# A short bias table read with overlapping rows, and forget-gated heads and pooling products over all 128 rows

## The chip, the core and the metric

The kernel runs on one core of one Trainium2 chip. The metric is the device time of one execution in microseconds (us); several runs are made, and their median counts.

## The reference, cut to what matters

The model is a chain of ten stages on 512 tokens of width 1024: an even mixer, memory cross-attention and feed-forward, then an odd mixer, cross-attention and feed-forward, and then twice a second kind of mixer (`mixer2`) with its feed-forward. The change touches three places.

The odd mixer has eight heads of dilated attention with three branches. The kernel merges them into one softmax over 512 keys, with a bias that depends on the head and on the distance between query and key alone:

```
bias = rel_bias[_t5_bucket(delta * dil)].transpose(2, 0, 1)
logits = jnp.where(valid, logits + bias, -jnp.inf)
```

In `mixer2` eight heads of 64 columns attend with forget gates, in query blocks of 128, each over the keys up to its own end:

```
logits = einsum('bhqd,bhkd->bhqk', qb, kb) * scale
logits = logits + (c[:, :, q0:q1, None] - c[:, :, None, :q1])
logits = jnp.where(causal, logits, -inf);  p = softmax(logits)
```

and four pooling groups of 64 columns each pass through a small product:

```
d = stack(groups, axis=2)                 # (b, s, 4, 64)
out = einsum('bsgc,gcd->bsgd', d, w_grp)  # 64 -> 256 per group
```

## The kernel before

All large products are float32 split in two float32r parts, a high one and a low one: `mm3` issues three products (high x high, high x low, low x high) for each 128-row piece (L246 to 251). `unit` (L206) is how weights come in: SP loads a block of 1024 columns by 128 rows into one of 3 raw buffers, ScalarE casts the high part (L167), VectorE subtracts it for the low part (L168), and the pairs have 5 buffers. SP's queue carries nearly all weight loads, in order; a load waits there until a raw buffer is free. POOL's queue carries the parked copy of X and small transfers. A scheduler orders the instructions of each engine ahead of time by its own model; each engine then runs its list in order and waits at semaphores. Products go to two PSUM tags, `mm` and `at`, with four banks each.

`bias_table` (L1110) runs in the first cross-attention (layer 0), between the products for the memory's keys and values and those for the queries. It multiplies a 33 x 640 one-hot matrix by the 33 x 8 bias rows (L1122), copies the 8 x 640 result to SBUF (L1123), and writes it to DRAM with each row repeated 128 times, one element further each time: 8 x 128 x 512. `odd_head` (L1214) reads 128 x 512 of it per head into `bt` (L1220, two buffers), and VectorE adds a slice of it to the logits and takes the maximum in one instruction (L1229).

In `mixer2` (L1248) the keys are projected first, then the queries. After each token tile `forget_k` (L1564) transposes it and writes, for even and odd heads (e = 0, 1), the high part into the 64 rows of that head and, by a copy on POOL's queue, into the other 64 rows as well. The low part goes into 64 rows of `kl` alone, even heads in one half of the rows and odd heads in the other. `forget_q` writes the query's high part into the head's own 64 rows and its low part into the other 64. So one product over 128 rows gives q_high k_high + q_low k_high, and a second one over 64 rows (L1607) gives q_high k_low. `forget_head` (L1591) adds per query block the gate sums (L1603), the causal mask as identity x mask in bfloat16 (L1604), and those two (L1606, L1607), with n = 128, 256, 384 or 512 columns, all into one bank. The head loop (L1316) issues for each head: its logits, a quarter of the short convolution's projection as filler, then the softmax and value products of the head before.

`gates` (L1369) computes the gate projections and adds the branches; the pooled values hold the high part in 64 rows and the low part in the other 64, and per output tile there is a product with the high weights over 128 rows (L1435) and one with the low weights over 64 rows (L1436).

Of the kernel before, what the change touches and what calls it, by code (L numbers as in the profile page):

```python
# [9 lines left out]
F32 = mybir.dt.float32  # L10
# [22 lines left out]
def constants():  # L33
# [31 lines left out]
    onehot[32] = np.where(ok, np.log(np.maximum(mult, 1)), NEG)  # L65
    c["c_onehot"] = onehot
    sel = np.zeros((P, 8, P), np.float32)
# [34 lines left out]
class Core:  # L102
# [1007 lines left out]
    def bias_table(self, xt):  # L1110
        nc, a = self.nc, self.a
        self.rel = self.dp.tile([8, P, S], F32, name="rel")
        with self.tc.tile_pool(name="rbp", bufs=1) as rp:
            rb = rp.tile([33, 8], F32, name="rb")
            nc.gpsimd.memset(rb[32:33, :], 1.0)
            nc.gpsimd.dma_start(out=rb[0:32, :], in_=a["rel_bias"])
            oh = xt.tile([P, 2, S], F32, tag="ph", name="oh", bufs=1).rearrange("p a b -> p (a b)")[:33, :640]
            nc.gpsimd.dma_start(out=oh, in_=a["c_onehot"])
            o = rp.tile([8, 640], F32, name="o")
            for c in range(2):  # L1120
                p = self.at_tile()
                nc.tensor.matmul(p[:8, :320], lhsT=rb, rhs=oh[:, c * 320:(c + 1) * 320], start=True, stop=True)  # L1122
                nc.vector.tensor_copy(out=o[:, c * 320:(c + 1) * 320], in_=p[:8, :320])  # L1123
            oo = o[:, 127:128]
            nc.gpsimd.dma_start(out=self.rel, in_=bass.AP(oo.tensor, oo.offset, [list(oo.ap[0]), [-1, P], [1, S]]))

# [87 lines left out]
    def odd_head(self, ot, kT, qT, vv, lows, h, stash):  # L1214
# [4 lines left out]
        bt = ot.tile([P, S], F32, tag="bt", name=self.nm("bt"))  # L1219
        nc.gpsimd.dma_start(out=bt, in_=self.rel[h])  # L1220
        pe = ot.tile([P, 1280], F32, tag="pe", name=self.nm("pe"))
        mx = self.small(4, "omx")
        den = self.small(4, "oden")
        for j in range(NT):
            n = (j + 1) * P
            p = self.at_tile()
            tq = slice(j * P, (j + 1) * P)
            self.mm3(p[:, :n], qT[:, hh, tq], lows["q"][:, hh, tq], kT[:, hh, :n], lows["k"][:, hh, :n], True, True)
            v.tensor_tensor_reduce(out=pe[:, koff[j]:koff[j] + n], in0=p[:, :n], in1=bt[:, (3 - j) * P:],  # L1229
                                   scale=1.0, scalar=-3.0e38, op0=ALU.add, op1=ALU.max, accum_out=mx[:, j:j + 1])  # L1230
# [17 lines left out]
    def mixer2(self, l, after):  # L1248
# [3 lines left out]
        with ExitStack() as st:  # L1252
# [5 lines left out]
            with tc.tile_pool(name=self.nm("fap"), bufs=1) as ap, tc.tile_pool(name=self.nm("fat"), bufs=2) as at:  # L1258
# [3 lines left out]
                nc.scalar.copy(out=sel.rearrange("r h p -> r (h p)"), in_=self_f[:, :D])  # L1262
                cau = ap.tile([P, P], BF16, name=self.nm("cau"))
                idb = ap.tile([P, P], BF16, name=self.nm("idb"))
                cf = at.tile([P, S], F32, tag="sq", name=self.nm("cf"), bufs=3)[:, :P]
# [7 lines left out]
                ks = [self.big(2, dt=F32R), ap.tile([P, 4, S], F32R, name=self.nm("fk"))]  # L1273
                kl = self.big(3, dt=F32R)
                q_end = []
# [40 lines left out]
                for h in range(8):  # L1316
                    fin = self.forget_head(at, ks[h % 2], kl, qs[h % 2], vv, h, cc, sel, cau, idb)

# [50 lines left out]
    def gates(self, mp, bt, l, w, aT, ds, ch, cl):  # L1369
# [24 lines left out]
        def pool_unit(fb):  # L1394
            rows = slice((fb % 2) * 64, (fb % 2) * 64 + 64)
            raw, hi, lo = [self.wp.tile([P, 1024], d, tag=t, name=self.nm("w"), bufs=n) for d, t, n in
# [3 lines left out]
            self.split(hi[:, :256], lo[:, :256], raw[:, :256])  # L1400
            return hi, lo[rows], rows

# [26 lines left out]
        def pool_conv(fb):  # L1429
            hi, lo, rows = feed.get()  # L1430

            def end(c, g, a_, u):
                f = fb * 2 + c
                p = self.at_tile()
                nc.tensor.matmul(p, lhsT=hi[:, c * P:(c + 1) * P], rhs=ds[:, fb, :], start=True, stop=False)  # L1435
                nc.tensor.matmul(p, lhsT=lo[:, c * P:(c + 1) * P], rhs=ds[rows, fb, :], start=False, stop=True)  # L1436
                nc.scalar.activation(out=g, in_=g, func=AF.Sigmoid)
# [126 lines left out]
    def forget_k(self, src, t, ks, kl, gain):  # L1564
# [5 lines left out]
        for e in range(2):  # L1570
            r, o = slice(e * 64, e * 64 + 64), slice(64 - e * 64, 128 - e * 64)
            hi = ks[e][r, :, cols]
            nc.scalar.activation(out=hi, in_=pt[r], func=AF.Copy, scale=gain[r])
            nc.vector.scalar_tensor_tensor(out=kl[r, :, cols], in0=pt[r], scalar=gain[r], in1=hi.bitcast(F32),
                                           op0=ALU.mult, op1=ALU.subtract)
            nc.gpsimd.dma_start(out=ks[e][o, :, cols], in_=hi)

    def forget_q(self, src, t, qs):
# [12 lines left out]
    def forget_head(self, at, kT, kl, qT, vv, h, cc, sel, cau, idb):  # L1591
# [3 lines left out]
        koff = (0, 128, 384, 768)  # L1595
        rows = slice((h % 2) * 64, (h % 2) * 64 + 64)
        pe = at.tile([P, 1280], F32, tag="pe", name=self.nm("pe"))
        mx = self.small(4, "fmx")
        den = self.small(4, "fden")
        for j in range(NT):  # L1600
# [5 lines left out]
            mm(p[:, :n], lhsT=qT[:, h // 2, tq], rhs=kT[:, h // 2, :n], start=False, stop=False)  # L1606
            mm(p[:, :n], lhsT=qT[rows, h // 2, tq], rhs=kl[rows, h // 2, :n], start=False, stop=True)  # L1607
            v.tensor_reduce(out=mx[:, j:j + 1], in_=p[:, :n], axis=AX.X, op=ALU.max, negate=True)
# [86 lines left out]
```

## Time and profile before

| what | value |
|---|---|
| runs | 3079.27, 3080.72, 3085.94 us (median 3080.72) |
| profiled execution | 3073.62 us, span 3071.8 us, mean granted TensorE clock 0.995 |
| busy: TensorE products | 3011.6 us, 98% of the span |
| busy: VectorE, ScalarE, POOL | 2264.3 (74%), 1512.4 (49%), 67.6 (2%) |
| moved by DMA | 317.42 MB, 103 GB/s on average |

An engine's busy time is the time its instructions run; idle time of an engine costs something only if the chain of work that ended last passes through it. PE stands for TensorE's products, PEld for its weight loads, DVE for VectorE, ACT for ScalarE, SPq and POOLq for the queues of SP and POOL. A product's recorded length holds its way through the array, so products overlap; their spacing is read from their starts or from the chain.

### The profile page before, as it was taken

How to read it: one execution, taken by the hardware profiler on the slowest of the kernel's cores; microseconds unless marked ns; L12 is line 12 of the kernel's file. 1: busy time of each engine (PE TensorE's matmuls, PEld its weight loads, DVE VectorE, ACT ScalarE, POOL GpSimd, SP SyncE). 2: the span in 40 equal slices, each digit the busy share in tenths (PEclk: the TensorE clock that was granted, in tenths of full speed). 3: DMA queues.
4: the chain of work that ended last, by engine and by line, in shares of the span. 5: the costliest groups of instructions: out<-in, count | busy, mean ns of one | idle time of the engine just before them, and what ended most of it. 6: DMA issues, size and time to landing. Idle time of an engine off the chain costs nothing.

```text
span 3071.8 us, 46569 instructions
## 1 busy us (share of the span) xinstructions
PE 3011.6 (98%) x18376; PEld 2612.7 (85%) x18376; DVE 2264.3 (74%) x4172; ACT 1512.4 (49%) x2475; POOL 67.6 (2%) x100
## 2 busy tenths in 40 slices
PE   8999979999999999999999999999999999999999
PEld 6888868899988788899988689899998769989998
DVE  6855746988777576888878588687777768778775
ACT  6634535554444454555454465454444445554442
POOL 1300000000000000000000000000001000000000
PEclk9999989999999999999999999999999999999999
DMA  5023632333332352232333032423234213423332
GB/s 186 30 83 96 181 91 72 111 109 98 104 110 89 110 178 83 90 117 90 111 125 100 27 119 86 157 77 117 90 109 120 86 55 107 150 71 110 110 103 76
DMA packets 229311, 317.42 MB, mean 103 GB/s; under 512 B 10813, under 2 KB 161839, under 8 KB 228197
## 3 DMA queue, kind: packets, MB, share of 16 engines
q1 hardware_dynamic: 220309, 290.08, 30.1%
q0 software_dynamic: 8784, 24.38, 2.9%
q8 instruction: 144, 2.36, 0.3%
q14 instruction: 74, 0.61, 0.1%
HBM read 294.49 MB, written 17.83 MB: 102 GB/s over the span
## 4 chain that ended last, share of the span: by engine, by line
PE 86%; DVE 7%; DMA 4%; ACT 2%; issue 1%; POOL 0%; SPq 0%; ACTq 0%; DVEq 0%
PE mm L248 58%; PE at L248 19%; PE at L203 3%; DVE wl L168 2%; PE at L1211 2%; DMA wr<-in_xa_w_o 1%; DVE wr L470 1%; PE at L1607 1%; DMA wr<-in_ffn_w_in 1%; PE at L1603 1%; ACT wh L167 1%; PE at L696 0%; PE at L1606 0%; DMA wr<-in_w_ffn_in 0%; PE at L853 0%
## 5 line engine op out<-in xcount | busy, mean ns | idle before, releaser
L168 DVE TENSOR_TENSOR wl<-wr,wh 128x1024 fp32r<-128x1024 f32 (+1 forms) x678 | 817.2, 1212 | 332.5 <-ACT wh L167 320.9
L167 ACT CAST wh<-wr 128x1024 fp32r<-128x1024 f32 (+1 forms) x678 | 700.6, 1042 | 545.2 <-PE mm L248 309.0
L248 PE MATMUL mm<-Hh,wh 128*128 128x256 f32 (+1 forms) x2256 | 679.7, 301 | 4.6 <-DVE u L529 2.4
L248 PE MATMUL mm<-Hh,wl 128*128 128x256 f32 (+1 forms) x2256 | 674.0, 299 | 0.0
L248 PE MATMUL mm<-Hl,wh 128*128 128x256 f32 (+1 forms) x2256 | 673.5, 299 | 0.0
L248 PEld LDWEIGHTS mm<-Hh,wh 128*128 128x128 f32 x2256 | 424.3, 188 | 31.0 <-issue 5.4
L248 PEld LDWEIGHTS mm<-Hl,wh 128*128 128x128 f32 x2256 | 424.5, 188 | 23.0 <-issue 5.3
L248 PEld LDWEIGHTS mm<-Hh,wl 128*128 128x128 f32 x2256 | 424.3, 188 | 20.4 <-issue 3.3
L248 PE MATMUL mm<-wh,Hh 128*128 128x512 f32 x896 | 359.1, 401 | 1.5 <-ACT Hh L167 1.5
L248 PE MATMUL mm<-wh,Hl 128*128 128x512 f32 x896 | 353.5, 396 | 0.8 <-DVE Hl L168 0.8
L248 PE MATMUL mm<-wl,Hh 128*128 128x512 f32 x896 | 353.0, 394 | 0.0
L248 PE MATMUL mm<-big,wh 128*128 128x256 f32 x1920 | 338.6, 279 | 4.2 <-ACT u L528 3.2
L248 PEld LDWEIGHTS mm<-big,wh 128*128 128x128 f32 x1920 | 289.7, 188 | 10.2 <-ACT u L528 4.2
L470 DVE TENSOR_TENSOR wr<-wr,wr 128x1024 f32<-128x1024 f32 x208 | 253.6, 1219 | 52.5 <-DMA wr<-in_w_ffn_in 27.4
L248 PE MATMUL at<-wh,al 128*128 128x512 f32 x704 | 277.4, 394 | 0.0
L248 PE MATMUL at<-wl,ah 128*128 128x512 f32 x704 | 276.0, 392 | 0.0
L248 PE MATMUL at<-wh,ah 128*128 128x512 f32 x704 | 273.6, 389 | 0.0
L248 PE MATMUL mm<-big,wl 128*128 128x256 f32 x960 | 265.4, 277 | 0.4 <-DVE wl L168 0.4
L248 PEld LDWEIGHTS mm<-wh,Hl 128*128 128x128 f32 x896 | 168.9, 189 | 40.2 <-DVE Hl L168 3.0
L248 PEld LDWEIGHTS mm<-wh,Hh 128*128 128x128 f32 x896 | 169.2, 189 | 36.1 <-ACT Hh L167 2.3
L248 PEld LDWEIGHTS mm<-wl,Hh 128*128 128x128 f32 x896 | 169.3, 189 | 34.6
L248 PEld LDWEIGHTS mm<-big,wl 128*128 128x128 f32 x960 | 180.1, 188 | 0.8 <-DVE wl L168 0.8
(408 smaller groups left out, 4334.7 us busy)
## 6 DMA issues: line engine op xcount, KB each, us to landing
wr<-in_ffn_w_in SPq DMA_DIRECT2D x88, 512.0 KB
wr<-in_w_ffn_in SPq DMA_DIRECT2D x88, 512.0 KB
wr<-in_w_in SPq DMA_DIRECT2D x84, 512.0 KB
wr<-in_ffn_w_out SPq DMA_DIRECT2D x44, 512.0 KB
wr<-in_w_ffn_out SPq DMA_DIRECT2D x44, 512.0 KB
wr<-in_ev_w_in SPq DMA_DIRECT2D x32, 512.0 KB
wr<-in_xa_w_kv SPq DMA_DIRECT2D x32, 512.0 KB
wr<-in_od_w_in SPq DMA_DIRECT2D x24, 512.0 KB
```

Source lines behind the costliest of these rows:

```text
L167: self.nc.scalar.copy(out=hi, in_=src)
L168: self.nc.vector.tensor_tensor(out=lo, in0=src, in1=hi.bitcast(F32), op=ALU.subtract)
L203: return self.nc.tensor.transpose(out=out, in_=in_, identity=self.ident)
L248: return self.nc.tensor.matmul(*args, **kw, skip_group_check=more)
L470: self.nc.vector.tensor_tensor(out=out, in0=a, in1=b, op=op)
L1211: nc.tensor.matmul(out[:, i * P:], lhsT=v[:, i, h * width:(h + 1) * width], rhs=pT[:, OFF[i]:OFF[i] + S - i * P], start=i == 0, stop=i == ...
L1603: mm(p[:, :n], lhsT=sel[:, h, :], rhs=cc[:, :n], start=True, stop=False)
L1607: mm(p[:, :n], lhsT=qT[rows, h // 2, tq], rhs=kl[rows, h // 2, :n], start=False, stop=True)
```

## The change

The one-hot matrix is stored reversed, so that the table comes out reversed. The 8 x 640 result itself goes to DRAM, on SP's queue, and each head reads 128 rows of 512 out of one row of 640, each row starting one element after the one before; VectorE reads the slice backwards. In `mixer2` the mask and identity become float32r. The low part of the keys now fills all 128 rows, in one set of tiles for even heads and one for odd heads; the odd set takes the two buffers of the tag `xn` that the normalisation uses between stages. `forget_k` computes each low part in two instructions of 256 columns and copies each to the other 64 rows with a DMA on SP's queue. The last product of each query block runs over 128 rows, which adds q_low k_low. In `pool_unit` and `pool_conv` the low weights are used over 128 rows, which adds low x low.

```diff
--- before.py
+++ after.py
@@ -63,7 +63,7 @@
     ok = (dist >= 0) & (mult > 0)
     onehot[bucket[ok], u[ok]] = 1.0
     onehot[32] = np.where(ok, np.log(np.maximum(mult, 1)), NEG)
-    c["c_onehot"] = onehot
+    c["c_onehot"] = np.ascontiguousarray(onehot[:, ::-1])
     sel = np.zeros((P, 8, P), np.float32)
     for h in range(8):
         sel[h, h] = -1.0
@@ -1109,7 +1109,7 @@
 
     def bias_table(self, xt):
         nc, a = self.nc, self.a
-        self.rel = self.dp.tile([8, P, S], F32, name="rel")
+        self.rel = self.dp.tile([8, 640], F32, name="rel")
         with self.tc.tile_pool(name="rbp", bufs=1) as rp:
             rb = rp.tile([33, 8], F32, name="rb")
             nc.gpsimd.memset(rb[32:33, :], 1.0)
@@ -1121,8 +1121,7 @@
                 p = self.at_tile()
                 nc.tensor.matmul(p[:8, :320], lhsT=rb, rhs=oh[:, c * 320:(c + 1) * 320], start=True, stop=True)
                 nc.vector.tensor_copy(out=o[:, c * 320:(c + 1) * 320], in_=p[:8, :320])
-            oo = o[:, 127:128]
-            nc.gpsimd.dma_start(out=self.rel, in_=bass.AP(oo.tensor, oo.offset, [list(oo.ap[0]), [-1, P], [1, S]]))
+            nc.sync.dma_start(out=self.rel, in_=o)
 
     def odd(self, after):
         nc, a, tc = self.nc, self.a, self.tc
@@ -1217,7 +1216,9 @@
         hh = h % 4
         koff = (0, 128, 384, 768)
         bt = ot.tile([P, S], F32, tag="bt", name=self.nm("bt"))
-        nc.gpsimd.dma_start(out=bt, in_=self.rel[h])
+
+        r0 = self.rel[h:h + 1, 1:2]
+        nc.gpsimd.dma_start(out=bt, in_=bass.AP(r0.tensor, r0.offset, [[1, P], [1, S]]))
         pe = ot.tile([P, 1280], F32, tag="pe", name=self.nm("pe"))
         mx = self.small(4, "omx")
         den = self.small(4, "oden")
@@ -1226,7 +1227,7 @@
             p = self.at_tile()
             tq = slice(j * P, (j + 1) * P)
             self.mm3(p[:, :n], qT[:, hh, tq], lows["q"][:, hh, tq], kT[:, hh, :n], lows["k"][:, hh, :n], True, True)
-            v.tensor_tensor_reduce(out=pe[:, koff[j]:koff[j] + n], in0=p[:, :n], in1=bt[:, (3 - j) * P:],
+            v.tensor_tensor_reduce(out=pe[:, koff[j]:koff[j] + n], in0=p[:, :n], in1=bt[:, :n][:, ::-1],
                                    scale=1.0, scalar=-3.0e38, op0=ALU.add, op1=ALU.max, accum_out=mx[:, j:j + 1])
         v.tensor_scalar(out=mx, in0=mx, scalar1=-1.0, scalar2=None, op0=ALU.mult)
         for j in range(NT):
@@ -1260,8 +1261,8 @@
                 self_f = at.tile([P, 1280], F32, tag="pe", name=self.nm("self"))
                 nc.gpsimd.dma_start(out=self_f[:, :D], in_=a["c_sel"].rearrange("r h p -> r (h p)"))
                 nc.scalar.copy(out=sel.rearrange("r h p -> r (h p)"), in_=self_f[:, :D])
-                cau = ap.tile([P, P], BF16, name=self.nm("cau"))
-                idb = ap.tile([P, P], BF16, name=self.nm("idb"))
+                cau = ap.tile([P, P], F32R, name=self.nm("cau"))
+                idb = ap.tile([P, P], F32R, name=self.nm("idb"))
                 cf = at.tile([P, S], F32, tag="sq", name=self.nm("cf"), bufs=3)[:, :P]
                 nc.gpsimd.dma_start(out=cf, in_=a["c_causal"])
                 nc.scalar.copy(out=cau, in_=cf)
@@ -1271,7 +1272,9 @@
 
                 qs = [self.big(1, dt=F32R), ap.tile([P, 4, S], F32R, name=self.nm("fq"))]
                 ks = [self.big(2, dt=F32R), ap.tile([P, 4, S], F32R, name=self.nm("fk"))]
-                kl = self.big(3, dt=F32R)
+                k0 = self.big(3, dt=F32R)
+                k1 = [self.tp.tile([P, 2, S], F32R, tag="xn", name=self.nm("kx")) for _ in range(2)]
+                kl = [[k0[:, 0:2], k0[:, 2:4]], k1]
                 q_end = []
                 for nme, base in (("k", S), ("q", 0)):
                     us = self.units_b(w, base)
@@ -1314,7 +1317,7 @@
                 aT = self.big(0)
                 fill, conv_out = self.short_conv(bt, w, l, cx)
                 for h in range(8):
-                    fin = self.forget_head(at, ks[h % 2], kl, qs[h % 2], vv, h, cc, sel, cau, idb)
+                    fin = self.forget_head(at, ks[h % 2], kl[h % 2][h // 4], qs[h % 2], vv, h, cc, sel, cau, idb)
 
                     def nxt(h=h, fin=fin):
                         if h % 2 == 0:
@@ -1392,13 +1395,12 @@
             return w[r * 512:r * 512 + 512, c0:c0 + 256]
 
         def pool_unit(fb):
-            rows = slice((fb % 2) * 64, (fb % 2) * 64 + 64)
             raw, hi, lo = [self.wp.tile([P, 1024], d, tag=t, name=self.nm("w"), bufs=n) for d, t, n in
                            ((F32, "raw", 3), (F32R, "whi", 5), (F32R, "wlo", 5))]
             for r in range(0, P, 64):
                 nc.sync.dma_start(out=raw[r:r + 64, :256], in_=a["pool_w_2"][l, fb])
             self.split(hi[:, :256], lo[:, :256], raw[:, :256])
-            return hi, lo[rows], rows
+            return hi, lo
 
         for fb in range(4):
             feed.put(lambda fb=fb: self.unit(a["w_conv_out_2"][l][:, fb * 256:fb * 256 + 256], 2, 256))
@@ -1427,13 +1429,13 @@
             return sg
 
         def pool_conv(fb):
-            hi, lo, rows = feed.get()
+            hi, lo = feed.get()
 
             def end(c, g, a_, u):
                 f = fb * 2 + c
                 p = self.at_tile()
                 nc.tensor.matmul(p, lhsT=hi[:, c * P:(c + 1) * P], rhs=ds[:, fb, :], start=True, stop=False)
-                nc.tensor.matmul(p, lhsT=lo[:, c * P:(c + 1) * P], rhs=ds[rows, fb, :], start=False, stop=True)
+                nc.tensor.matmul(p, lhsT=lo[:, c * P:(c + 1) * P], rhs=ds[:, fb, :], start=False, stop=True)
                 nc.scalar.activation(out=g, in_=g, func=AF.Sigmoid)
                 v.tensor_tensor(out=m[f], in0=m[f], in1=g, op=ALU.mult)
                 sg = second(a_, u)
@@ -1571,9 +1573,12 @@
             r, o = slice(e * 64, e * 64 + 64), slice(64 - e * 64, 128 - e * 64)
             hi = ks[e][r, :, cols]
             nc.scalar.activation(out=hi, in_=pt[r], func=AF.Copy, scale=gain[r])
-            nc.vector.scalar_tensor_tensor(out=kl[r, :, cols], in0=pt[r], scalar=gain[r], in1=hi.bitcast(F32),
-                                           op0=ALU.mult, op1=ALU.subtract)
             nc.gpsimd.dma_start(out=ks[e][o, :, cols], in_=hi)
+            for i in range(2):
+                lo = kl[e][i][r, :, cols]
+                nc.vector.scalar_tensor_tensor(out=lo, in0=pt[r, i * 2:i * 2 + 2], scalar=gain[r],
+                                               in1=hi[:, i * 2:i * 2 + 2].bitcast(F32), op0=ALU.mult, op1=ALU.subtract)
+                nc.sync.dma_start(out=kl[e][i][o, :, cols].bitcast(F32), in_=lo.bitcast(F32))
 
     def forget_q(self, src, t, qs):
         nc = self.nc
@@ -1593,7 +1598,6 @@
         v = nc.vector
         mm = nc.tensor.matmul
         koff = (0, 128, 384, 768)
-        rows = slice((h % 2) * 64, (h % 2) * 64 + 64)
         pe = at.tile([P, 1280], F32, tag="pe", name=self.nm("pe"))
         mx = self.small(4, "fmx")
         den = self.small(4, "fden")
@@ -1604,7 +1608,7 @@
             mm(p[:, j * P:n], lhsT=idb, rhs=cau, start=False, stop=False)
             tq = slice(j * P, (j + 1) * P)
             mm(p[:, :n], lhsT=qT[:, h // 2, tq], rhs=kT[:, h // 2, :n], start=False, stop=False)
-            mm(p[:, :n], lhsT=qT[rows, h // 2, tq], rhs=kl[rows, h // 2, :n], start=False, stop=True)
+            mm(p[:, :n], lhsT=qT[:, h // 2, tq], rhs=kl[:, h // 2 % 2, :n], start=False, stop=True)
             v.tensor_reduce(out=mx[:, j:j + 1], in_=p[:, :n], axis=AX.X, op=ALU.max, negate=True)
             nc.scalar.activation(out=pe[:, koff[j]:koff[j] + n], in_=p[:, :n], func=AF.Exp,
                                  bias=mx[:, j:j + 1], accum_out=den[:, j:j + 1])
```

## Rows read from the trace of the kernel before

**Rows 1.** The chain of work that ended last, by engine

```profile
PE 86%; DVE 7%; DMA 4%; ACT 2%; issue 1%; POOL 0%; SPq 0%; ACTq 0%; DVEq 0%
```

**Rows 2.** The chain in the first cross-attention: start us, us, what

```profile
349.26 0.44 PE at L203 x4
...
360.71 1.17 PE at L1122 x4
...
372.66 36.50 DMA wr<-in_xa_w_o
...
466.17 3.96 PE mm L248 x17
```

**Rows 3.** The chain in the second cross-attention

```profile
1120.69 0.44 PE at L203 x4
...
1213.92 6.27 PE mm L248 x27
```

**Rows 4.** Windows: us, busy of PE, PEld, DVE, ACT, POOL, PEclk, DMA share, GB/s

```profile
349.26:466.17 116.91, 97.17 (x487) 80.07 (x485) 58.24 (x143) 45.54 (x84) 1.09 (x1) 0.91 0.45 108
...
1120.69:1213.92 93.23, 93.23 (x483) 77.95 (x481) 57.77 (x141) 44.54 (x84) 0.00 (x0) 1.00 0.35 113
1600.00:1650.00 50.00, 49.92 (x239) 40.79 (x238) 46.09 (x147) 28.49 (x45) 8.34 (x15) 1.00 0.51 140
1689.00:1775.00 86.00, 85.75 (x373) 52.83 (x372) 45.97 (x106) 34.85 (x93) 0.00 (x0) 1.00 0.10 32
...
1870.00:1927.00 57.00, 56.27 (x467) 53.70 (x465) 47.40 (x60) 32.21 (x52) 0.00 (x0) 1.00 0.34 101
```

**Rows 5.** The chain through one head's logits

```profile
1695.81 0.06 PE at L1603
...
1699.01 0.42 PE at L1607
1699.43 2.99 PE mm L248 x12
```

**Rows 6.** The chain: like products in a row

```profile
1661.21 27.99 PE mm L248 x120
...
1702.43 1.09 PE at L203 x10
```

**Rows 7.** The timeline of PEld: start us, us, instruction [idle before]

```profile
1688.34 0.19 PEld L248 LDWEIGHTS mm<-wl,Hh 128*128 128x128 f32 x1
...
1692.33 0.18 PEld L1607 LDWEIGHTS at<-big,big 64*128 64x128 f32 x1 [0.24 <-issue]
```

**Rows 8.** DMA issues: size and median us to landing

```profile
xd<-x POOLq DMA_DIRECT2D x5, 2048.0 KB, 8.6
...
rel<-o POOLq DMA_DIRECT2D x1, 2048.0 KB, 45.5
bt<-rel POOLq DMA_DIRECT2D x8, 256.0 KB, 3.4
...
fk<-fk POOLq DMA_DIRECT2D x8, 128.0 KB, 2.9
```

**Rows 9.** The timeline of the queues of SP and POOL

```profile
347.99 17.17 SPq L211 DMA_DIRECT2D wr<-in_xa_w_q  x8
...
363.44 1.09 POOL L1125 DMA_DIRECT2D rel<-o  x1 [48.09 <-DVE o L1123]
```

**Rows 10.** Groups by line and shape: count | busy us, mean ns

```profile
L993 DVE SCALAR_TENSOR_TENSOR kl<-at,gv,big 128x256 fp32r<-128x256 f32 x16 | 7.6, 477 | 0.1
...
L1574 DVE SCALAR_TENSOR_TENSOR big<-at,gv,fk 64x512 fp32r<-64x512 f32 x8 | 6.1, 756 | 0.3
```

**Rows 11.** The timeline of the odd mixer's third head: bias read and first use

```profile
927.66 0.54 POOL L1220 DMA_DIRECT2D bt<-rel  x1 [73.30 <-DVE omx L1229]
...
937.39 0.29 DVE L1229 CUSTOM_DVE_ANT_0 pe<-at,bt 128x128 f32<-128x128 f32 x1 [1.43 <-PE at L248]
```

**Rows 12.** The chain at a pooling product

```profile
1815.83 0.42 PE at L1436
```

## The prediction

> **What bounds the kernel now.** I read first the chain of work that ended last: TensorE carries 86% of the span [rows 1]. So an edit is worth what it takes off TensorE, or off a wait that TensorE has; work added to VectorE, ScalarE or a queue costs only where its cover ends. The profiled execution took 3073.6 us (span 3071.8 and 1.8 around it); the median of the runs is 3080.7, 7.1 higher. I work the sum out against the execution and put it on the median.
>
> Next I looked for the diff's lines in the chain. Two stand out. In the first cross-attention, where the bias table is built, the chain holds 36.5 us of a weight transfer [rows 2]. The second cross-attention is the same code without the table, and its chain holds no transfer there [rows 3]. The windows by stage say the same: 97.2 of 116.9 us busy on TensorE in the one, 93.2 of 93.2 in the other [rows 4]. Then the forget-gated heads: TensorE is busy there from end to end, VectorE and ScalarE about half [rows 4], and the products of 64 rows (L1607) and those just ahead of them take longer than their columns [rows 5, 6, 7].
>
> **The table's write.** Removed: one POOL write of 2048 KB from 8 partitions, 45.5 us to land, while parking X moves as many bytes in 8.6 us [rows 8]. It is issued at 363.4 us [rows 9], so it lands at 408.9. The weight block on the chain lands at 372.66 + 36.50 = 409.16 [rows 2], in the same instant: the load stood behind the write. What that cost is read between two marks that both cross-attentions have, the transposes of the last key tile but one and the start of the output product. First: 466.17 - 349.26 = 116.91. Second: 1213.92 - 1120.69 = 93.23. Difference 23.68, which holds the clock lost after the idle stretch as well (granted 0.91 of full speed on average against 1.00 [rows 4]). The table's own products (L1122, 1.17) stay [rows 2]. Gain 23.68 - 1.17 = 22.5 us. Bounds: nothing, if another transfer takes the wait over, and 23.7.
>
> Added: 20 KB on SP's queue. It waits for VectorE's copy of the table (the old write started right behind that, at 363.4), and the weight loads of the next projection that come later in SP's order wait behind it. Query's first product starts at 361.9 [rows 2]. If every load stood behind the copy, the first weights would land at 363.4 + 3.4 [rows 8] = 366.8, and VectorE's split of the 1024-column block takes, by estimate from a 256-column subtraction, 4 x 0.48 = 1.9 [rows 10]: some 7 us late. Loads ahead of it make that nothing, and SP issues the loads of this projection from 348.0 on [rows 9], so I take 0 and keep +7.
>
> **Reading the table.** Eight reads stay on POOL, 256 KB each, 3.4 us to land [rows 8]; now all 128 rows come out of one 2.5 KB line of DRAM. The third read is issued at 927.66 and used at 937.39 [rows 11], a cover of 9.7 us; four of the eight have that or a little more, the others far more. Nothing in the trace reads overlapping rows, so the bounds are 0 and a landing longer than the cover (a rival). Reading the bias backwards in VectorE: same instruction, same elements, 0; no row shows it.
>
> **The heads.** 2 layers x 8 heads x 4 query blocks, four products each. In the chain a head takes 1699.43 - 1695.81 = 3.62 us for its sixteen products [rows 5]. The 512-column product of 64 rows takes 0.42 [rows 5] where a product of 512 columns in a row of like ones takes 27.99 / 120 = 0.233 [rows 6]. The load of weights says why: the 64-row load starts only after 0.24 us of idle array, while a 128-row load between two full products has none [rows 7]. Coming back from 64 to 128 rows costs about the same again, so there are two such gaps per block. After the edit all four are 128-row float32r. I price them by the rate in a row: 0.233, 0.175 and 0.117 for 512, 384 and 256 columns, and 1.09 / 10 = 0.109 for 128 columns, the transposes' rate, since the load then sets the pace [rows 6]. Blocks: 4 x 0.109 = 0.44; 3 x 0.117 + 0.109 = 0.46; 3 x 0.175 + 0.109 = 0.63; 3 x 0.233 + 0.109 = 0.81; sum 2.34. Gain 3.62 - 2.34 = 1.28 per head, x 16 = 20.5 us. Bounds: if one of the two gaps stayed in each block (0.42 - 0.233 = 0.19; at the mask product, or waiting for a bank), 64 x 0.19 = 12 less, 8; if 128 columns cost only their columns (0.058), 16 x 4 x 0.05 + 16 x 3 x 0.05 = 6 more, 26. The mask product going from bfloat16 to float32r is inside these numbers. VectorE needs 45.97 / 8 = 5.7 us per head, ScalarE 4.4, TensorE 10.75 now and 9.5 after [rows 4]: still TensorE.
>
> A rule speaks against this term. The Trainium skill, page "TensorE: Matmul & The Clock Gate", section "The mechanism", says that a weight load overlaps running products only when their row groups differ. By it, full products in a row would expose every load, and the heads and pooling would gain nothing. The load rows of this trace do not agree: 0 idle between full products [rows 7].
>
> **The pooling products.** 16 of them: 0.42 becomes 0.233 [rows 6, 12], 0.19 x 16 = 3.0 us. In the middle of the gates (1870 to 1927, half of these products) TensorE is 56.3 of 57 busy [rows 4] but the chain runs over VectorE and weight loads; there the gain may go into the next wait. I take 2, bounds 0 and 3.
>
> **The key's low part.** Per call (8 calls) two subtractions of 512 columns become four of 256: 2 x 0.48 in place of about 0.75 [rows 10], so +0.2 x 16 = 3.2 us of VectorE, under a TensorE that is 49.9 of 50 busy there; VectorE has 46.1 of 50 [rows 4], so the cover is 3.9 us per 50 and the eight of one layer take 1.6 of it. Added too: 4 copies per call on SP, 32 in all, each behind its subtraction, with the loads of the query, value and gate weights queued behind. Like copies on POOL take 2.9 us to land [rows 8], and the first head is 45 us later. Bounds 0 and 3.2 for VectorE; I take +1 for both, and the queue is a rival.
>
> **Sum.** -22.5 - 20.5 - 2 + 1 = -44. Execution: 3029.6. Median: 3080.7 - 44 = 3036.7, so 3037. Its own range, from the bounds: lower end -23.7 - 26 - 3 + 0 = -53, 3028; upper end -22.5 + 7 - 8 - 0 + 3 = -20.5, 3060. Bounds seldom fall together, so for the likeliest case alone 3028 to 3050.
>
> **The rivals.**
> A, the heads gain nothing (0.10). The loads stay exposed as the rule above would have it, or query blocks wait for one of the four PSUM banks that VectorE and ScalarE must clear. For it: odd heads have a bank less, the accumulator's. Against: [rows 7] and half-idle engines [rows 4]. -22.5 - 0 - 0 + 1: 3059.
> B, the 36.5 us stall stays, since it was not the write (0.05). For it: the row names a weight block, not the table. Against: both land together, and the second cross-attention has no stall. -21.5: 3059.
> C, the overlapping read is slow, the side that ends slower (0.06). For it: 128 rows out of one 2.5 KB line, nothing like it in the trace. Four reads have 9.7 us of cover [rows 11]; each microsecond of landing beyond that costs 4 us. The gain of 44 is gone at 9.7 + 11 = 20.7 us, and by 22.3 the kernel is 6 us slower. Against: 3.4 us now, and even the write from 8 partitions ran at 46 GB/s, which gives 5.6 us.
> D, SP's new copies hold the weight loads (0.08). If each of the 8 calls delays TensorE by a copy's landing, 2.9 us [rows 8], +23: 3060. Against: SP mostly sits in waits for VectorE that come just as late.
> The forecast itself has 0.71.
>
> **How the numbers follow.** Range 3026 to 3060: it holds the forecast, A and B whole, and about half of D, and leaves out C and the rest, some 0.1 to 0.15. What a measurement can tell from no change is 0.2%, 6 us. Faster: forecast, A, B, D, 0.94. C gives 0.04 slower and 0.02 within 0.2%.
>
> **What would show each step.** Right: no transfer on the chain of the first cross-attention, its stretch near 94.4 us with clock 1.00; the table's write in a few us; L1607 with 128 rows and no idle time before its load, a head's sixteen products in about 2.3 us, the heads' stage 10 us shorter per layer; the bias reads under 9 us to land. Wrong: a transfer ahead of query's products, VectorE waiting for the bias tile at L1229 and its like, TensorE waiting at the k and q projections for split weights, or idle time before the loads of the heads' products.

## The result

The changed kernel takes 3036.65 us (median of four runs, 3036.28 to 3037.10) beside 3079.99 us for the kernel before, run beside it (3076.74 to 3085.94): a ratio of 0.9857, 95% interval 0.984 to 0.9874, a gain of 43.3 us. Forecast were 3037 us and a gain of 44. In a later comparison (the run e9 below) the same kernel came to 0.9854 [0.9837, 0.987].

The two profiled executions lie closer together than the medians: 3073.62 before, 3036.64 after, 37.0 us. Where the other 6 us are is a finding of its own, below.

### The profile page after: what moved, and what is told of

It is laid out like the page before. It is cut to its first block, busy times and chain, and to the rows that moved or that the text cites. A ratio compares the mean times of both kernels' runs of the same rounds, so it can differ in the third digit from the quotient of the medians.

```text
span 3034.9 us, 46642 instructions
## 1 busy us (share of the span) xinstructions
PE 2985.4 (98%) x18376; PEld 2613.1 (86%) x18376; DVE 2265.0 (75%) x4188; ACT 1512.8 (50%) x2475; POOL 66.5 (2%) x99
## 4 chain that ended last, share of the span: by engine, by line
PE 85%; DVE 9%; DMA 3%; ACT 2%; issue 1%; POOL 0%; SPq 0%; DVEq 0%; ACTq 0%
PE mm L248 58%; PE at L248 19%; PE at L203 3%; DVE wl L168 2%; PE at L1210 2%; DVE wr L470 1%; DMA wr<-in_w_ffn_in 1%; DMA wr<-in_ffn_w_in 1%; DMA wr<-in_w_in 1%; ACT wh L167 1%; PE at L696 0%; PE at L853 0%; DMA wr<-in_w_o 0%; DVE big L168 0%; DVE x L546 0%
```

## The profile after

The chain of work that ended last, by engine, beside [rows 1]: a share of DMA is gone, one of VectorE has come.

```profile
PE 85%; DVE 9%; DMA 3%; ACT 2%; issue 1%; POOL 0%; SPq 0%; DVEq 0%; ACTq 0%
```

The chain in the first cross-attention, between the marks of [rows 2]:

```profile
350.84 0.44 PE at L203 x4
351.27 11.01 PE mm L248 x48
362.29 1.17 PE at L1122 x4
363.45 16.99 PE mm L248 x72
...
445.47 4.66 PE mm L248 x20
```

From the table's products (L1122) the chain goes on at once into 72 products and never leaves TensorE; the 36.50 us of the weight transfer are not there. Between the marks lie 445.47 - 350.84 = 94.63 us, where there were 116.91.

The timeline of SP's queue in the same stretch shows what the new write stands between:

```profile
349.33 14.40 SPq L211 DMA_DIRECT2D wr<-in_xa_w_q  x7
364.79 0.30 SPq L1124 DMA_DIRECT2D rel<-o  x1
366.28 0.37 SPq L211 DMA_DIRECT2D wr<-in_xa_w_q  x1
```

Seven of the eight weight loads of the query projection are issued ahead of it, and only the last one behind, 1.5 us later. The bias reads, in the list of DMA issues (beside [rows 8]):

```profile
bt<-rel POOLq DMA_DIRECT2D x8, 256.0 KB, 4.1
```

And the instructions that use the bias tile, with the shortest, middle and longest ns of one and the waits:

```profile
L1230 DVE CUSTOM_DVE_ANT_0 pe<-at,bt x32: 282/488/693, 904.2 to 1016.6; 128x128 f32<-128x128 f32 x8, 128x256 f32<-128x256 f32 x8, 128x384 f32<-128x384 f32 x8, 128x512 f32<-128x512 f32 x8
...
  POOL bt L1221: 3.0, 1
DMA to landing us min/median/max: 3.3/4.1/10.5
```

A read lands in 4.1 us (it was 3.4), once in 10.5. That one is the second read, issued at 832.4 us right behind POOL's parking of X, and it is used 75 us later; in the kernel before the second read took 9.1. Only POOL's own queue waited for a read, 3.0 us; no VectorE instruction did, and one with the slice read backwards takes what it took (the same line before: 279/486/692).

Now the stages of `mixer2`, each between two places in the program that both kernels have. Windows of the kernel before, with the columns of [rows 4]: the projections of keys and queries up to the last but three tiles, the heads, the gates, and the heads of the second layer.

```profile
1610.39:1655.18 44.79, 44.79 (x211) 36.67 (x210) 41.66 (x129) 20.73 (x31) 4.94 (x8) 1.00 0.45 112
1661.21:1774.87 113.66, 113.41 (x492) 75.20 (x491) 67.21 (x126) 47.38 (x108) 1.11 (x2) 1.00 0.15 48
1796.77:1944.56 147.79, 145.82 (x1121) 136.37 (x1121) 124.67 (x159) 82.27 (x134) 0.00 (x0) 1.00 0.40 123
2397.53:2511.17 113.64, 113.40 (x493) 75.20 (x491) 67.20 (x126) 47.40 (x108) 1.11 (x2) 1.00 0.15 48
```

The same of the changed kernel, with the first cross-attention ahead of them:

```profile
350.84:445.47 94.63, 94.63 (x486) 78.17 (x485) 58.18 (x143) 45.81 (x84) 0.00 (x0) 1.00 0.34 112
1589.23:1633.97 44.74, 44.74 (x210) 36.66 (x210) 42.15 (x136) 20.73 (x31) 4.92 (x8) 1.00 0.56 135
1640.00:1743.28 103.28, 102.31 (x492) 74.72 (x491) 66.68 (x126) 46.97 (x108) 1.11 (x2) 1.00 0.17 53
1765.17:1913.21 148.04, 143.17 (x1121) 136.52 (x1121) 124.66 (x159) 82.21 (x134) 0.00 (x0) 1.00 0.39 123
2367.12:2470.71 103.59, 102.66 (x492) 74.83 (x491) 66.71 (x126) 46.96 (x108) 1.11 (x2) 1.00 0.17 53
```

The heads went from 113.66 to 103.28 and from 113.64 to 103.59: 20.4 us together. The gates, with the pooling in them, did not get shorter: TensorE is busy 2.65 us less (145.82 to 143.17), but its idle time grew from 1.97 to 4.87. The stage with the new copies on SP is as long as before.

In the timeline of the weight loads, the load of the last product (now L1611) has no idle time before it, against 0.24 us in [rows 7]; within a query block of few columns the loads follow one another every 0.11 to 0.12 us:

```profile
1667.57 0.19 PEld L1610 LDWEIGHTS at<-big,big 128*128 128x128 f32 x1
1667.68 0.19 PEld L1611 LDWEIGHTS at<-big,big 128*128 128x128 f32 x1
1667.80 0.19 PEld L1607 LDWEIGHTS at<-cc,sel 128*128 128x128 f32 x1
```

So of the 37.0 us between the two executions, 22.3 lie in the first cross-attention and 20.4 in the heads, 42.7 in all, and something else gave back 5.7.

## The experiments

**The kernel before again, and each half of the change alone.** e1 is the kernel before, unchanged, for the question what two executions of one program differ by (its answer stands in the next section). e2 has the table's edit alone:

```diff
-        self.rel = self.dp.tile([8, P, S], F32, name="rel")
+        self.rel = self.dp.tile([8, 640], F32, name="rel")
...
-            nc.gpsimd.dma_start(out=self.rel, in_=bass.AP(oo.tensor, oo.offset, [list(oo.ap[0]), [-1, P], [1, S]]))
+            nc.sync.dma_start(out=self.rel, in_=o)
...
+        r0 = self.rel[h:h + 1, 1:2]
+        nc.gpsimd.dma_start(out=bt, in_=bass.AP(r0.tensor, r0.offset, [[1, P], [1, S]]))
```

e3 has the keys' low part over 128 rows alone, with the mask left in bfloat16:

```diff
-            mm(p[:, :n], lhsT=qT[rows, h // 2, tq], rhs=kl[rows, h // 2, :n], start=False, stop=True)
+            mm(p[:, :n], lhsT=qT[:, h // 2, tq], rhs=kl[:, h // 2 % 2, :n], start=False, stop=True)
```

e4 has the float32r mask alone, with the products of 64 rows left as they were:

```diff
-                cau = ap.tile([P, P], BF16, name=self.nm("cau"))
-                idb = ap.tile([P, P], BF16, name=self.nm("idb"))
+                cau = ap.tile([P, P], F32R, name=self.nm("cau"))
+                idb = ap.tile([P, P], F32R, name=self.nm("idb"))
```

> The kernel before, unchanged, for a second profile of it. In its first profile the feed-forward products of 256 columns ran at 19.29 us per 168, in that of after at 19.29 to 19.95, which makes the four feed-forward stages 8.1 us longer after. My theory: that pace differs from execution to execution and has nothing to do with the edits; then some blocks of 168 here take 19.4 to 19.8 as well, and the span is 2 to 8 us above 3071.8. Rival: the edits slowed it; then all blocks take 19.29 here and the span is 3070 to 3073. Time: same as before.

> The kernel before with the short table alone (write of 20 KB on SP, overlapping reads, backward slice); heads and pooling as before. My theory: the stall of the first cross-attention goes and nothing else changes: 22 us off, about 3057, and the stretch of 116.9 us becomes 94.2. Rival, that the stall was only the slowest of several waits there: 5 to 15 us off.

> The kernel before with the keys' low part over 128 rows alone (new tiles, copies on SP, no 64-row product); mask and identity stay bfloat16, table and pooling as before. My theory, that the two gaps at the 64-row product are the whole gain: a head's sixteen products take 2.3 to 2.7 us in place of 3.62, 15 to 21 us off in all, 3059 to 3065. Rival, that the change of type at the mask product carries half of it: 8 to 11 us off.

> The kernel before with mask and identity in float32r alone; the 64-row products stay. My theory: what is won by not changing type (0.11 us at three of four blocks) is lost again on the slower load: within 3 us of before. Rival: each change of type costs a gap of its own, 64 x 0.1 to 0.2 us = 6 to 12 us off.

Beside 3074.73 us for the kernel before (19 runs, 3071.17 to 3080.42):

| run | median us | ratio, 95% interval |
|---|---|---|
| e1, before again | 3074.90 | 1.0 [0.9991, 1.001] |
| e2, table only | 3053.44 | 0.9927 [0.9912, 0.9942] |
| e3, heads only | 3051.70 | 0.9922 [0.9905, 0.9938] |
| e4, mask type only | 3077.30 | 1.0007 [0.9998, 1.0017] |

e2 and e3 each give about half: 21.3 and 23.0 us, in all 44.3, and the whole change gave 43.3 in its own comparison, so the halves add up and neither hides the other. The 23.0 of e3 is more than the 15 to 21 expected of it; why is shown in the next section. The type of the mask alone gives nothing (the ratio holds 1); what the heads gained came from the rows. The chain of e3 through one head's sixteen products shows it without a break (start us, us, what), to be held against [rows 5]:

```profile
1693.57 0.06 PE at L1607
1693.63 0.07 PE at L1608
1693.70 0.12 PE at L1610
...
1695.11 0.24 PE at L1607
...
1695.42 0.29 PE at L1610
1695.70 0.23 PE at L1611
1695.94 2.80 PE mm L248 x12
```

1695.94 - 1693.57 = 2.37 us where it was 3.62; in the block of 512 columns the last product takes 0.23 instead of 0.42. In e4 the same head still takes 1697.41 - 1693.79 = 3.62.

**Which property of the old write held the weights back.** e5 is the changed kernel with the old write of 2048 KB put beside the new one; nothing reads it.

```diff
             nc.sync.dma_start(out=self.rel, in_=o)
+            big = self.dp.tile([8, P, S], F32, name="relbig")
+            oo = o[:, 127:128]
+            nc.gpsimd.dma_start(out=big, in_=bass.AP(oo.tensor, oo.offset, [list(oo.ap[0]), [-1, P], [1, S]]))
```

e6 writes as many bytes in the same place, but from 128 partitions; the short table goes on POOL's queue, and the large write right behind it.

```diff
-            nc.sync.dma_start(out=self.rel, in_=o)
+            r = nc.gpsimd.dma_start(out=self.rel, in_=o)
+            big = self.dp.tile([P, 8, S], F32, name="relbig")
+            with self.tc.issue_after(r.ins):
+                nc.gpsimd.dma_start(out=big, in_=self.Hh.bitcast(F32))
```

> The changed kernel with, beside its short table, the old write of 2048 KB from 8 partitions by POOL at its old place, into a tensor that nobody reads. My theory, that this write alone held the weight load: the first cross-attention is back at some 117 us and the time is 20 to 25 us above that of after (3057 to 3061 where before takes 3080). Rival, that the wait came with the way that the table was built or read: no change, within 3 us of after.

> The changed kernel with the short table written by POOL and behind it, on the same queue at the same moment, 2048 KB from 128 partitions into a tensor that nobody reads. Theory one, that the source of 8 partitions made the old write slow and so the stall long: it lands in 8 to 12 us, the first cross-attention stays within 5 us of 94, within 5 us of after. Theory two, that 2 MB at this moment are too much from any source, because the weights are due then: 15 us or more above after.

Beside 3073.59 us for the kernel before (7 runs, 3066.92 to 3079.42), e5 takes 3052.50 us, 0.9926 [0.9901, 0.9952], and e6 3028.95, 0.9856 [0.9838, 0.9875]. The changed kernel's ratio of 0.9857 would be 3029.6 here, so the old write costs 22.9 us when it comes back, and the wide one nothing. The chain of e5 has the old row again, on the same weight:

```profile
374.90 36.51 DMA wr<-in_xa_w_o
```

and its window between the marks is 117.17 us with TensorE busy 97.44, as in [rows 4]; e6's window is 94.62:

```profile
351.51:468.68 117.17, 97.44 (x486) 80.25 (x485) 57.89 (x142) 45.65 (x84) 1.09 (x1) 0.91 0.44 107
```

```profile
348.82:443.44 94.62, 94.62 (x487) 78.19 (x485) 58.01 (x142) 45.78 (x84) 1.04 (x2) 1.00 0.39 133
```

The large write in the DMA issues of e6, with KB and us to landing, and then the issue of e5's write and its landing:

```profile
relbig<-Hh POOLq DMA_DIRECT2D x1, 2048.0 KB, 7.9
```

```profile
L1127 POOL DMA_DIRECT2D relbig<-o x1: 1093/1093/1093, 365.7 to 365.7; - x1
...
DMA to landing us min/median/max: 45.4/45.4/45.4
```

In e5 the write is issued at 365.7 us and lands at 411.1, the weight at 374.90 + 36.51 = 411.41: again in the same instant. So it was the write, and of the write not its bytes but its form.

The packets of the two queues show how (packets, MB, and the time that they took as a share of 16 DMA engines; the write's queue, POOL's, is software_dynamic, the weights' queue, SP's, is hardware_dynamic). First e5 from 385 to 400 us, then e6 from 365 to 370:

```profile
q0 software_dynamic: 177, 0.72, 46.5%
q1 hardware_dynamic: 177, 0.18, 3.4%
```

```profile
q0 software_dynamic: 125, 1.88, 100.9%
```

A packet of the old write takes 0.465 x 16 x 15 / 177 = 0.63 us and holds 4 KB, one of the wide write takes 1.009 x 16 x 5 / 125 = 0.65 us and holds 15 KB on average; the old write keeps 0.465 x 16 = 7.4 engines busy, the wide one all 16. So the old form is slow twice over: about a quarter of the bytes in each packet, and half as many packets at a time. The weights beside it get one packet of 1 KB for each packet of the write, 177 and 177 (179 and 178 in the kernel before): they do not stop, they creep at 0.18 MB in 15 us, 12 GB/s. By their size these are packets of the query projection's last block (256 columns in a row), which SP issued before the block that the chain names; SP's queue, too, waits for it in e5 (us in total, times, longest):

```profile
SPq L211 <- DMA wr<-in_xa_w_q: 24.5, 1, 24.5
```

So the block on the chain came behind a block that crept beside the write. The sources of the two forms differ in their partitions (8 and 128) and in the length of the pieces read there (512 elements, each piece one element further, against whole rows of 4096); which of the two makes the packets small and which keeps engines idle, these runs don't part.

**The pooling, and the type of the mask.** e7 is the changed kernel with the pooling products of 64 rows back:

```diff
-            return hi, lo
+            return hi, lo[(fb % 2) * 64:(fb % 2) * 64 + 64]
...
-                nc.tensor.matmul(p, lhsT=lo[:, c * P:(c + 1) * P], rhs=ds[:, fb, :], start=False, stop=True)
+                nc.tensor.matmul(p, lhsT=lo[:, c * P:(c + 1) * P], rhs=ds[(fb % 2) * 64:(fb % 2) * 64 + 64, fb, :], start=False, stop=True)
```

e8 is the changed kernel with the two lines of e4's diff the other way round, mask and identity in bfloat16.

> The changed kernel with the pooling products of 64 rows put back (low x low left out, as in the kernel before). My prediction took 2 us for them. By the profile of after, TensorE is idle 4.9 us in the gates where it was idle 2.0 before, so what the products gave went into waits for weights: then the gates take as long as in after (within 1 us per layer) and the time is within 3 us of after. If the prediction's term was right: 2 to 3 us above.

> The changed kernel with mask and identity left in bfloat16. The heads alone with the bfloat16 mask made the stage with the heads 102.1 us, the changed kernel 103.3 and 103.6. Theory, that the slower load of the float32r identity is what is left: 1.2 us per layer, 2 to 3 us below after. Rival, that the difference is the order in which the scheduler puts the filler: nothing, or either sign.

In the comparison of e5 and e6, e7 takes 3029.81 us, 0.9857 [0.9836, 0.9878]: the ratio of the changed kernel. The pooling's edit is worth nothing that this can tell. Its window of the gates, between the places of the windows above, and then that of the changed kernel in a second execution (e9 below):

```profile
1763.43:1910.32 146.89, 145.38 (x1122) 136.03 (x1121) 124.76 (x159) 82.62 (x134) 0.00 (x0) 1.00 0.39 124
```

```profile
1761.29:1907.30 146.01, 142.43 (x1122) 136.08 (x1121) 124.69 (x159) 82.16 (x134) 0.00 (x0) 1.00 0.39 124
```

With 64 rows TensorE is busy 145.38 of 146.89 us, idle 1.51; with 128 rows 142.43 of 146.01, idle 3.58. Of the 2.95 us that the products give, 2.07 come back as waiting. TensorE's waits in the two windows (us in total, times, longest), e7 first, say at what: at ScalarE's copies out of PSUM (`us`, L528).

```profile
PE mm L248 <- ACT u L528: 0.4, 1, 0.4
```

```profile
PE mm L248 <- ACT u L528: 2.6, 3, 1.1
```

And the chain of e9 at one of them says what the copy itself comes behind: a weight load and ScalarE's cast of that weight. At another, at 1863 us, the chain runs over a weight load (3.68 us) and VectorE's split.

```profile
1884.21 4.30 DMA wr<-in_w_o
...
1888.59 1.05 ACT wh L167
1889.63 0.28 ACT u L528
```

e8 takes 3026.30 us, 0.9847 [0.9828, 0.9865], 3 us below e6 and e7, and its heads' stages are 102.08 and 102.10 us instead of 103.28 and 103.59. To see whether that is a better version, both were run side by side, the changed kernel as e9 and the one with the bfloat16 mask as e10.

> The changed kernel as it is. Beside the kernel before its ratio was 0.9857 [0.984, 0.9874]; the same ratio is expected here, 0.984 to 0.9875. For the profile: the two heads' stages 103.3 to 103.6 us each as in the first profile of it, if those lengths belong to the order of the work in it; 102.1 in one of them would say that 1.2 to 1.5 us of them was chance. In the four feed-forward stages the blocks of products of 256 columns should show a mixture of 19.29 and longer, not the same mixture as in the first profile, if the pace differs from execution to execution.

> The changed kernel with the mask and the identity left in bfloat16 (the output is the reference's to the rounding of the type; the products with 128 rows of keys stay). Theory: the bfloat16 mask makes the heads' stages 102.1 us instead of 103.3 to 103.6, so 2.4 to 3.0 us of the whole, a ratio to the kernel before 0.0008 to 0.0010 lower than that of the changed kernel in the same call. Rival: the 3 us of the first comparison lay within the spread of that chip, and the two come out within 0.0003 of one another, though the stages differ.

e9 takes 3026.20 us (3023.87 to 3027.23), 0.9854 [0.9837, 0.987]; e10 takes 3026.43 (3024.20 to 3027.08), 0.9852 [0.9837, 0.9867]. The stages differ as they did: TensorE is busy 102.68 of 103.61 us in e9's first heads and 101.84 of 102.09 in e10's, and so in the second layer:

```profile
1635.79:1739.40 103.61, 102.68 (x492) 74.81 (x491) 66.72 (x126) 46.93 (x108) 1.11 (x2) 1.00 0.16 53
2359.18:2462.47 103.29, 102.33 (x492) 74.74 (x491) 66.70 (x126) 46.93 (x108) 1.11 (x2) 1.00 0.17 53
```

```profile
1638.14:1740.23 102.09, 101.84 (x492) 72.19 (x491) 66.70 (x126) 46.80 (x109) 1.11 (x2) 1.00 0.17 53
2360.10:2462.19 102.09, 101.84 (x493) 72.19 (x491) 66.69 (x126) 46.81 (x109) 1.11 (x2) 1.00 0.17 53
```

So the stage is 1.2 to 1.5 us shorter with bfloat16, in four of four stages of e8 and e10. Whether that is the identity's slower load alone is open: the order of TensorE's products in the stage is not the same in e9 and e10 either, and e8's rival, the scheduler's order, was not tested by itself. And the medians of e9 and e10 differ by only 0.2 us. Each kernel's runs spread over 3 us, as much as the 2.4 to 3.0 us in question; no version was found that measurably beats the changed kernel.

## Why the prediction was right, and where its terms were off

**The table's write: 22.5 forecast; 22.3 in the profile, 21.3 in e2, 22.9 put back in e5.** The step that named the write as what held the weight is shown by e5 and e6 together: the write back brings the row back, and its bytes in another form do not. That fells rival B. Only "stood behind" is not exact: the load stood behind another weight block, and that one ran beside the write, one small packet for each of the write's. The +7 for SP's order fell away for the reason that the prediction gave as possible: seven of the eight loads are issued ahead of the copy.

**Reading the table: 0 forecast, 0 found.** Landing took 4.1 us in the middle, longer than the 3.4 of whole rows but under the 9.7 us of cover [rows 11]; the four reads with little cover took 4.1 to 4.4, and the longest, 10.5, had 75 us. Rival C needed 20.7 us. (Its estimate from the old write, 45.5 / 8, is 5.7 us and not 5.6.) The backwards slice costs nothing: 488 ns against 486.

**The heads: 20.5 forecast, 20.4 in the profile, 23.0 in e3.** That the 64-row products were the cost is shown by e3 and e4. That the number came out so close is partly luck, since two terms that it lacked nearly cancel. The price list made from [rows 6] gave 2.34 us for a head's sixteen products; e3 shows 2.37, and the first head of each layer in the changed kernel takes 2.35 by the starts of its products. But the 3.62 us of [rows 5] end where the next products begin, and so leave out the last return from 64 rows to 128: the twelve products behind the head take 2.99 there and 2.80 in e3. That is 0.19 x 16 = 3.0 us of gain not counted, and 16 x (3.62 - 2.37) + 3.0 = 23.0 is what e3 has. Against it, the mask's new type was put inside these numbers without a price of its own: with float32r the stage holds 0.5 to 0.8 us more of TensorE's busy time and 0.7 us more idle, 2.4 to 3.0 us in the two layers. A smaller detail cancels within the head: the load was to set a pace of 0.109 for each product of 128 columns, but in e3, where the mask is bfloat16, its product takes 0.07 and the one behind it 0.05 to 0.06 more than its columns (0.29 at 512). And the 0.24 us of [rows 7] are idle time in the weight loads' own timeline; no view shows idle time of the array there, so the gap is to be read from the spacing of the products. Rival A, that loads stay exposed, would have left 113.6 us; the loads of L1611 have no idle time before them. So the rule of the Trainium skill (page "TensorE: Matmul & The Clock Gate", section "The mechanism"), by which a load overlaps running products only where the row groups differ, does not hold for these products. The runs show the opposite order: the products that change from 128 rows to 64 and back expose their loads.

**The pooling: 2 forecast, 0 measured.** This is the term that was mis-sized, twice. The busy time that it frees is larger than was priced, 2.65 to 2.95 us for the eight products of a layer, 0.33 to 0.37 each instead of 0.19, since the product after a 64-row one is delayed too, a gap that the prediction counted inside the heads and forgot here. By the starts of the products, the step from the 64-row product to the next is 0.42 to 0.43 us in e7 (but for the layer's first, which also waits) and 0.24 in e9, and the step after that 0.22 to 0.23 and about 0.12. But the stage is at the end of its cover: the weight loads, and the casts, splits and copies that come behind them on ScalarE and VectorE, take 2.1 to 2.9 us of it back as TensorE's waits; what is left, under 1 us a layer (146.01 against 146.89, but 148.04 against 147.79 in the first pair), is too little for the runs to tell. The prediction named that wait and still took 2 of 3.

**The keys' low part: +1 forecast, 0 found.** The stage takes 44.74 us against 44.79, TensorE busy throughout. VectorE's busy time rose by 0.49 us and the DMA share from 0.45 to 0.56, both under cover; rival D's 23 us are not there. The pooling's 2 and this +1, both not found, leave the forecast sum 1 us too high.

**The execution and the median.** The sum was made against one execution (3073.6) and put on the median. By the profiled executions alone the gain would read 37.0 us, 6 too few. The place is the feed-forward, which the change does not touch. The later part of the chain in each of its four stages holds equal blocks of 168 products of 256 columns; from the start of the first block to the end of the last, these parts are 1.48, 2.02, 2.82 and 1.77 us longer in the changed kernel's first profile, 8.1 together, of which other stretches gave some back. In the first profile of the changed kernel:

```profile
594.56 19.43 PE mm L248 x168
625.00 19.79 PE mm L248 x168
655.78 19.43 PE mm L248 x168
...
716.99 19.29 PE mm L248 x168
```

In that of the kernel before, all nine such blocks that were read in the same stretches of the program take 19.29. But e1, the kernel before once more, has these:

```profile
647.46 19.29 PE mm L248 x168
677.73 19.43 PE mm L248 x168
708.17 19.79 PE mm L248 x168
```

and e9, the changed kernel once more, has nine of nine at 19.29, where a mixture was expected; its span is 3022.1 us, 12.8 less than in its first profile. e1's span, 3072.8, is only 1.0 above that of the first profile of the kernel before, where 2 to 8 was expected. So both paces occur in both programs and the edit does not set them; whether the chip has a part in it is not shown. The medians and their ratio are therefore what the gain is to be read from. What sets the pace was not found.

## What to carry to other kernels

Before pricing a stall by the transfer that the chain names, look for another transfer that lands in the same instant, and look at its form: a write from few partitions in short pieces slowed a weight load of another queue to 12 GB/s, where the same bytes in another form cost nothing. A product of 64 rows between products of 128 costs two exposed loads, one going in and one coming out, so filling the unused rows is nearly free and pays where TensorE sets the end; where the weights and their splitting are close behind it, most of the gain turns into waiting. When a span of the trace is priced, look at the product behind its end as well: a gap can fall there. Add a profile-to-profile difference up by stage before believing its total, and check stages that were not touched.

## What the runs showed of the hardware that was not expected

- The same 2048 KB to DRAM took 45.4 to 45.5 us out of 8 partitions in overlapping pieces of 512 elements and 7.9 out of 128 partitions, and beside the slow one a load on another queue got one packet of 1 KB for each packet of 4 KB of the write (177 and 177 in 15 us of e5).
- Reading 128 overlapping rows of 2 KB out of 2.5 KB of DRAM lands in 3.8 to 4.1 us in the middle (e5, e6 and the changed kernel), against 3.4 for 128 rows of their own in the kernel before.
- Blocks of 168 products of 256 columns mostly take 19.29, 19.43 or 19.79 us (0.115 to 0.118 us each) in executions of the same kernel; the longer ones too stood in an execution whose mean granted clock was 1.000 (the changed kernel's first profile).
- The identity's load takes 96 ns in bfloat16 and 189 in float32r; alone, beside products of 64 rows, that changed nothing (e4).
